# The first MLP product of a float32 encoder trunk: hi and lo activations as one 512-column moving operand, with one PSUM bank for each 128 features

## The chip, the cores and the metric

The kernel runs on one core of one Trainium2 chip. The metric is the device time of one execution in microseconds (us); smaller is better. TensorE is called PE in the rows below (PEld is its weight loading), VectorE is DVE, ScalarE is ACT, GpSimd is POOL and SyncE is SP.

## The reference

Two layers run on 256 tokens of 2048 features, all in float32. The attention part is cut here to its frame; what the change is about is the first product of the MLP, `h @ w_up`, and the square that follows it.

```python
for l in range(DEPTH):                                  # DEPTH = 2
    h = rmsnorm(x, norm_mix[l])
    proj = jnp.einsum('bsd,de->bse', h, w_in[l])
    ...                                                 # three attention groups A, B, C on parts of proj
    x = x + jnp.einsum('bse,ed->bsd', mix, w_o[l])
    h = rmsnorm(x, norm_mlp[l])
    u = jax.nn.relu(jnp.einsum('bsd,df->bsf', h, w_up[l]))      # 2048 -> 8192
    x = x + jnp.einsum('bsf,fd->bsd', u * u, w_down[l])         # 8192 -> 2048
return rmsnorm(x, norm_final)
```

## The kernel before

Every dense product is made exact enough by splitting both factors into two fp32r parts, hi and lo, and by summing three products: hi\*hi, hi\*lo and lo\*hi. Weights stream from memory in tiles of 512 KB (`wraw`, 6 buffers). ACT casts a tile to `whi` (L783), DVE subtracts to get `wlo` (L784); each of the two has four buffers. One such tile is one "step" of the program, and the steps form one long list that PE works through.

A step of the input projection, the output projection or the second MLP product (`mode_b`, L446 to L448) makes 12 matmuls of 512 columns: the activations stand in the array, and 512 columns of weights move. A step of the first MLP product (`up_steps`) is the other way round: 128x128 blocks of weights stand in the array, and the transposed activations of all 256 tokens move, so that the result comes out transposed, as the second product needs it. The activations of two blocks of 128 features lie in one tile `ht` of shape [128, 2 (hi, lo), 2 (block kk), 256 tokens]. For each block kk and each group `fs` of 128 output features there are three matmuls of 256 columns: hi weights by hi activations (L611), hi weights by lo activations (L612) and lo weights by hi activations (L613). That makes 24 matmuls in a step. Eight steps finish a chunk of 512 output features, which is held in two PSUM banks (two groups `fs` share a bank). At the end of a chunk each bank is emptied: ACT takes the relu (L617), POOL squares (L618), ACT casts the hi part (L621), and DVE subtracts to get the lo part (L622).

A layer has 16 chunks of the first product, hence 128 steps; the order is two chunks of the first product (16 steps), then 16 steps of the second product that use the results of the two chunks before, and so on. The two layers have 2 x 16 x 8 = 256 steps of the first product, with 256 x 8 = 2048 groups of three matmuls.

PSUM has eight banks. Six of them form one pool, `bank`, for matmul results and transposes; the two others hold the tile `S` of the attention scores (L318). What each engine does is in program order on that engine; the order is set when the program is built, by a scheduler that takes buffers from free pools. Attention pieces (scores, transposes of the weights L362, products with the values) are slipped in between dense steps by a planner with fixed costs and delays, which the change leaves as they are.

Of the kernel before, what the change touches and what calls it, by code (L numbers as in the profile page):

```python
"""Hybrid encoder trunk (three attention groups, squared-ReLU MLP) on one core.

Dense products run on the tensor engine as float32 split exactly into two fp32r
parts (hi + lo); hi*hi + hi*lo + lo*hi carries float32's accuracy in three passes.
The residual stream, attention and normalisations stay on chip; only weights stream.
"""
# [27 lines left out]
OUT_ORDER = "ACB"  # L34
# mixer feature blocks of 256 (two k-blocks each): A 0-1, B 2-3, C 4-7
GROUP_BLOCKS = {"A": (0, 1), "B": (2, 3), "C": (4, 5, 6, 7)}
# [7 lines left out]
def tile_trunk(ctx: ExitStack, tc: tile.TileContext, x_in, w_in, w_o, w_up, w_down,  # L44
# [28 lines left out]
    def mm_bank():  # L73
        return pp.tile([P, 512], F32, tag="bank", bufs=6, name=nm("mm"))

    def tr_bank():
        return pp.tile([P, 512], F32, tag="bank", bufs=6, name=nm("tr"))

# [1 line left out]
    ident = cp.tile([P, P], F32, name="ident")  # L80
# [25 lines left out]
    def setup_tables():  # L106
        """Rope tables with the gains folded in: out = x * ctab + swap16(x) * stab."""
        nc.vector.tensor_scalar(negsink, rp[:, :, 0:8], -1.0, None, op0=ALU.mult)
        for l in range(L):
            nc.vector.tensor_scalar(rp[:, l, 8:72], rp[:, l, 8:72], 0.125, None, op0=ALU.mult)  # L110
            for which, off in (("q", 8), ("k", 72)):
                g = rp[:, l:l + 1, off:off + 64]
                c = cp.tile([P, NT, 64], F32, name=f"ctab_{which}{l}")
                s = cp.tile([P, NT, 64], F32, name=f"stab_{which}{l}")
                nc.vector.tensor_mul(c, cos_t, g.to_broadcast([P, NT, 64]))
                for a in range(4):
                    b = a ^ 1
                    nc.vector.tensor_mul(s[:, :, 16 * a:16 * a + 16], sin_t[:, :, 16 * a:16 * a + 16],
                                         g[:, :, 16 * b:16 * b + 16].to_broadcast([P, NT, 16]))
                ctab[which, l], stab[which, l] = c, s  # L120

    def setup_avec():
        """Relative-position vector of group A, reversed: avec[h, i] = bias(h, rel = 255 - i)."""
        t5x = cp.tile([33, 8], F32, name="t5x")
# [12 lines left out]

# [1 line left out]
    bgq = []  # L139
# [7 lines left out]
    def add(fn, cost, after=(), delay=0):  # L147
        """Queue fn, `cost` us of PE time; it may start `delay` us from now or after the pieces in `after`."""
        p = Piece()
        p.fn, p.cost, p.after, p.delay, p.at, p.done = fn, cost, after, delay, cur[0], None  # L150
        bgq.append(p)
        return p
# [23 lines left out]

# [1 line left out]
    def hprep(key, gcol, j, hT, ss, done, fin_rs, late=0):  # L178
        """Column chunk j of x: partial sums of squares; k-blocks 4j..4j+3 of the operand."""
        def sq():  # L180
# [56 lines left out]

# [1 line left out]
    def q_transposes(src, pr0, qT):  # L239
        """src [P, t, heads*64]; 4 heads from pair pr0 -> qT [hi;lo, 4, 256]."""  # L240
        ps = tr_bank()
# [12 lines left out]
    def k_transposes(src, pr0, npr, kh, kl):  # L254
        """src [P, t, heads*64]; head pairs pr0.. -> hi/lo [every head in both halves, heads, 256]."""
        ps = tr_bank()
# [12 lines left out]
    def v_split(ps, parts, t, r):  # L269
        """Value columns of one bank, scaled, as hi/lo; parts: (first column, heads, tile)."""  # L270
        src = [ps[:, c0:c0 + nh * 64].rearrange("p (h d) -> p h d", h=nh) for c0, nh, _ in parts]
# [6 lines left out]
    def rope(raw, H, which, l, outs):  # L278
        """raw [P, t, H, 64]: per-head RMS norm, gain and axial rotary, in place of outs(t)."""
        n = NT * H  # L280
# [21 lines left out]

# [1 line left out]
    class Unit:  # L304
# [4 lines left out]
    def queue_unit(u, *preps):  # L309
        """Scores, transposes of the weights, product with the values; spaced for the softmax between."""  # L310
        after = list(preps) + last_s[-1:]
        sc = add(lambda: unit_scores(u), 0.87, after=after, delay=[D_S] * len(preps) + [D_SS])
        tr = add(lambda: unit_transp(u), 0.87, after=(sc,), delay=(D_T,))
        add(lambda: unit_pv(u), 0.87, after=(tr,), delay=(D_PV,))
        last_s.append(sc)

    def unit_scores(u):
        S = pp.tile([P, 4, 256], F32, tag="S", bufs=1, name=nm("S"))  # L318
        for s in range(4):
            qh, kh, qb = u.slot(s)  # L320
            st = u.qT[:, qh, qb * P:(qb + 1) * P]
            nc.tensor.matmul(S[:, s, :], st, u.kh[:, kh, :], start=True, stop=False)  # L322
            nc.tensor.matmul(S[:, s, :], st, u.kl[:, kh, :], start=False, stop=True)  # L323
        p = big(F32, 4, 256)
# [3 lines left out]
        if u.kind == "C":  # L328
            nc.vector.tensor_reduce(negm, S, axis=AX.X, op=ALU.max, negate=True)
            src = S  # L330
        else:
            for b in range(2):
                nc.vector.scalar_tensor_tensor(p[:, 2 * b:2 * b + 2, :], S[:, 2 * b:2 * b + 2, :], 0.125,
                                               u.bias(b), op0=ALU.mult, op1=ALU.add)
# [4 lines left out]
            else:  # L339
                nc.vector.tensor_reduce(negm, p, axis=AX.X, op=ALU.max, negate=True)  # L340
            src = p
        for s in range(4):
            nc.scalar.activation(p[:, s, :], src[:, s, :], AF.Exp, bias=negm[:, s:s + 1],
                                 accum_out=sums[:, s:s + 1])
# [53 lines left out]
    def mix_prep(l, grp, blk, raw, mixT, sqacc, done):  # L398
        """A finished block of 256 features: gained hi/lo operand and sum of squares."""
        m = big(F32R, 2, 2, 256)  # L400
# [30 lines left out]

# [1 line left out]
    steps = []  # L433
# [5 lines left out]
    def mode_b(banks, h_tile, wh, wl, sub, first, last, n=512, blocks=(0, 1)):  # L439
        """out[tok, n] += operand^T W over the tile's k-blocks."""  # L440
        for t in blocks:
# [10 lines left out]
    def layer_steps(l):  # L452
# [10 lines left out]

        # -- input projection --
        def proj_evac(name, banks):
# [93 lines left out]

        # -- output projection --  # L560
        st["hT2"], st["ss2"] = [None] * 8, small(8)
# [26 lines left out]

        # -- MLP --
        uT = {}  # L590

        def up_steps(g):
            for c in range(2):
                fc = 2 * g + c
                box = {}
                for k in range(8):
# [3 lines left out]
                    def mm(wh, wl, k=k, fc=fc, box=box):  # L600
                        if k == 0:
                            box["b"] = [mm_bank(), mm_bank()]
                        ht = st["hT2"][k]
                        for kk in range(2):
                            for fs in range(4):
                                o = box["b"][fs // 2][:, (fs % 2) * 256:(fs % 2) * 256 + 256]
                                s0 = k == 0 and kk == 0 and fs % 2 == 0
                                s1 = k == 7 and kk == 1
                                sh = wh[:, kk, fs * P:(fs + 1) * P]
                                sl = wl[:, kk, fs * P:(fs + 1) * P]  # L610
                                nc.tensor.matmul(o, sh, ht[:, 0, kk, :], start=s0, stop=False, skip_group_check=True)  # L611
                                nc.tensor.matmul(o, sh, ht[:, 1, kk, :], start=False, stop=False, skip_group_check=True)  # L612
                                nc.tensor.matmul(o, sl, ht[:, 0, kk, :], start=False, stop=s1, skip_group_check=True)  # L613
                        if k == 7:
                            for b in range(2):
                                a = mid(F32, 512)
                                nc.scalar.activation(a, box["b"][b], AF.Relu, bias=zero1[:, 0:1])  # L617
                                nc.gpsimd.tensor_mul(a, a, a)  # L618
                                u = big(F32R, 2, 2, 256)
# [54 lines left out]
    def final_chunk(j):  # L674
        """Squares of a finished column chunk; the final gain goes in ahead of the scale."""
        if not fin:
# [14 lines left out]
    def final_block(t):  # L691
        """Last chunk of token block t: norm over the whole row, scale, store."""
        square(3, t)
# [12 lines left out]

# [1 line left out]
    def bias_a(kv):  # L708
# [57 lines left out]

# [1 line left out]
    raw_t, hi_t, lo_t = {}, {}, {}  # L768
# [110 lines left out]
def _pack(w, nk):  # L879
    """[K, n] -> tiles [K/(128 nk), 128, nk*n]."""  # L880
    K, n = w.shape
# [61 lines left out]
```

## Time and profile before

| | |
|---|---|
| median of 3 runs | 2088.51 us (2088.35 to 2090.66) |
| span of the profiled execution | 2088.3 us |
| PE busy | 2066.0 us, 99% of the span |
| DVE busy | 1273.8 us, 61% |
| ACT busy | 1041.4 us, 50% |
| POOL busy | 340.1 us, 16% |
| mean granted TensorE clock | 0.997 of full speed |

The profiled execution's span lies 0.2 us below the median of the timed runs, so a time worked out from the span can be read as a time of a run. Matmuls are pipelined and overlap in the profile: a row says 0.28 us or 0.39 us for one, and the next starts much earlier. What a matmul costs is read from the starts of neighbouring rows, not from its length.

### The profile page before, as it was taken

What the parts mean: (1) busy time and instruction counts of PE and PEld (TensorE: products, weight loads), DVE (VectorE), ACT (ScalarE), POOL (GpSimd) and SP (SyncE); (2) the same over time, 40 slices, a digit from 0 to 9 for tenths busy, and PEclk for the clock granted to TensorE, in tenths of its full rate; (3) what the DMA queues carried; (4) which work ended last, traced back from release to release, by engine and by line L of the source; (5) the groups of instructions that cost most, each with busy time, mean ns of one, the idle gap of its engine ahead of it and who ended that gap; (6) DMA issues with size and microseconds to landing.
All of it is one profiled execution on the core that took longest, in us unless ns stands there. A gap on an engine that the chain in (4) does not pass through costs nothing.

```text
span 2088.3 us, 31322 instructions
## 1 busy us (share of the span) xinstructions
PE 2066.0 (99%) x12444; PEld 1847.9 (88%) x12444; DVE 1273.8 (61%) x1426; ACT 1041.4 (50%) x1472; POOL 340.1 (16%) x362
## 2 busy tenths in 40 slices
PE   9999999999999999999999999999999999999998
PEld 7878889989899898998888788899899898999986
DVE  6777976454555545555668789754555545555555
ACT  6657755444344444434556566554344444434444
POOL 0484420000000000000005844101000000000001
PEclk9999999999999999999999999999999999999999
DMA  8545455565655656556556453555655656565563
GB/s 289 179 160 157 155 185 176 183 192 180 194 186 187 192 183 192 187 188 189 188 177 188 141 170 130 180 174 181 194 188 183 192 189 191 184 192 185 190 212 121
DMA packets 107550, 381.49 MB, mean 183 GB/s; under 512 B 11875, under 2 KB 14691, under 8 KB 107404
## 3 DMA queue, kind: packets, MB, share of 16 engines
q1 hardware_dynamic: 107116, 378.45, 56.6%
q8 instruction: 97, 1.59, 0.3%
q10 hardware_dynamic: 288, 1.05, 0.1%
q14 instruction: 49, 0.40, 0.1%
HBM read 377.34 MB, written 2.11 MB: 182 GB/s over the span
## 4 chain that ended last, share of the span: by engine, by line
PE 94%; POOL 2%; DVE 1%; ACT 1%; issue 1%; DMA 0%; SPq 0%; POOLq 0%; DVEq 0%
PE mm L446 18%; PE mm L447 18%; PE mm L448 18%; PE mm L612 12%; PE mm L613 12%; PE mm L611 12%; PE tr L362 1%; PE tr L192 1%; PE tr L381 1%; PE S L323 1%; PE S L322 1%; POOL big L300 1%; POOL big L506 0%; PE tr L245 0%; POOL sm L235 0%
## 5 line engine op out<-in xcount | busy, mean ns | idle before, releaser
L784 DVE TENSOR_TENSOR wlo<-wraw,whi 128x1024 fp32r<-128x1024 f32 (+1 forms) x697 | 863.4, 1241 | 697.4 <-ACT whi L783 695.0
L783 ACT CAST whi<-wraw 128x1024 fp32r<-128x1024 f32 (+1 forms) x697 | 729.9, 1048 | 884.6 <-PE mm L448 473.0
L446 PE MATMUL mm<-whi,big 128*128 128x512 f32 (+1 forms) x1792 | 695.7, 389 | 3.1 <-DVE big L252 3.1
L447 PE MATMUL mm<-wlo,big 128*128 128x512 f32 (+1 forms) x1792 | 693.0, 387 | 0.0
L448 PE MATMUL mm<-whi,big 128*128 128x512 f32 (+1 forms) x1792 | 692.4, 386 | 0.0
L611 PE MATMUL mm<-big,whi 128*128 128x256 f32 x2048 | 579.8, 283 | 0.0
L613 PE MATMUL mm<-big,wlo 128*128 128x256 f32 x2048 | 579.6, 283 | 0.0
L612 PE MATMUL mm<-big,whi 128*128 128x256 f32 x2048 | 579.6, 283 | 0.0
L446 PEld LDWEIGHTS mm<-whi,big 128*128 128x128 f32 x1792 | 337.8, 189 | 68.1 <-issue 3.4
L448 PEld LDWEIGHTS mm<-whi,big 128*128 128x128 f32 x1792 | 337.4, 188 | 68.0
L447 PEld LDWEIGHTS mm<-wlo,big 128*128 128x128 f32 x1792 | 337.9, 189 | 64.8 <-DVE wlo L784 0.2
L612 PEld LDWEIGHTS mm<-big,whi 128*128 128x128 f32 x2048 | 393.2, 192 | 0.5
L611 PEld LDWEIGHTS mm<-big,whi 128*128 128x128 f32 x2048 | 393.1, 192 | 0.5
L613 PEld LDWEIGHTS mm<-big,wlo 128*128 128x128 f32 x2048 | 393.1, 192 | 0.0
L618 POOL TENSOR_TENSOR mid<-mid 128x512 f32<-128x512 f32 x64 | 74.2, 1159 | 1247.3 <-ACT mid L617 1247.3
L353 POOL TENSOR_SCALAR big<-big,sm 128x256 f32<-128x256 f32 x128 | 87.5, 701 | 230.3 <-DVE sm L351 164.3
L643 DVE SCALAR_TENSOR_TENSOR x<-mm,sm,x 128x512 f32<-128x512 f32 x128 | 89.9, 744 | 4.5 <-PE mm L448 4.5
L622 DVE TENSOR_TENSOR big<-mid,big 128x512 fp32r<-128x512 f32 x64 | 44.1, 689 | 50.7 <-ACT big L621 50.7
L621 ACT CAST big<-mid 128x512 fp32r<-128x512 f32 x64 | 39.8, 621 | 50.7 <-POOL mid L618 50.7
L617 ACT ACTIVATE mid<-mm,zero 128x512 f32<-128x512 f32 x64 | 43.8, 684 | 39.5 <-PE mm L613 39.5
L235 POOL TENSOR_TENSOR sm<-sm,mhalf 128x2 f32<-128x2 f32 (+3 forms) x16 | 24.7, 1547 | 131.0 <-DVE sm L230 117.0
L364 DVE TENSOR_TENSOR big<-tr,big 128x512 fp32r<-128x512 f32 x64 | 41.1, 680 | 0.3
(117 smaller groups left out, 1013.2 us busy)
## 6 DMA issues: line engine op xcount, KB each, us to landing
wraw<-in_w_up_dram SPq DMA_DIRECT2D x256, 512.0 KB, 4.3
wraw<-in_w_down_dram SPq DMA_DIRECT2D x256, 512.0 KB, 4.1
wraw<-in_w_in_dram SPq DMA_DIRECT2D x120, 512.0 KB, 3.3
wraw<-in_w_o_dram SPq DMA_DIRECT2D x64, 512.0 KB, 3.6
biasB<-in_rpb_dram SPq DMA_DIRECT2D x16, 349.5 KB, 6.2
biasA<-avec SPq DMA_DIRECT2D x4, 768.0 KB, 4.9
x<-in_x_dram SPq DMA_DIRECT2D x3, 512.0 KB, 9.1
big<-in_gfin_dram SPq DMA_DIRECT2D x2, 512.0 KB, 4.3
```

What stands on the lines that cost most here:

```text
L353: nc.gpsimd.tensor_scalar(p[:, s, :], p[:, s, :], rs[:, s:s + 1], 1.0, op0=ALU.mult, op1=ALU.mult)
L446: nc.tensor.matmul(o, a_h, wh[:, i, :], start=first and i == 0, stop=False)
L447: nc.tensor.matmul(o, a_h, wl[:, i, :], start=False, stop=False)
L448: nc.tensor.matmul(o, a_l, wh[:, i, :], start=False, stop=last and i == len(sub) - 1)
L611: nc.tensor.matmul(o, sh, ht[:, 0, kk, :], start=s0, stop=False, skip_group_check=True)
L612: nc.tensor.matmul(o, sh, ht[:, 1, kk, :], start=False, stop=False, skip_group_check=True)
L613: nc.tensor.matmul(o, sl, ht[:, 0, kk, :], start=False, stop=s1, skip_group_check=True)
L618: nc.gpsimd.tensor_mul(a, a, a)
L622: nc.vector.tensor_sub(uf[:, 1, :], a, f(uf[:, 0, :]))
L643: nc.vector.scalar_tensor_tensor(xs, box["b"][t], st["r2"][:, t:t + 1], xs, op0=ALU.mult, op1=ALU.add)
L783: last_hi[0] = nc.scalar.copy(h[:, part], w[:, part]).ins
L784: nc.vector.tensor_sub(lo[:, part], w[:, part], f(h[:, part]))
```

## The change

The two matmuls with the same hi weights (L611 and L612) become one: the hi and lo activations move as one operand of 2 x 256 columns, out of `ht[:, :, kk, :]`, whose two runs of 256 columns lie 512 elements apart. The result is 512 columns wide and fills a bank: columns 0 to 255 collect hi\*hi, columns 256 to 511 collect hi\*lo. The third matmul (lo weights by hi activations) is as before and adds to columns 0 to 255. So each `fs` has a bank of its own, a chunk has four banks, and the two halves of a bank are added at the end. ACT copies one half out, DVE adds the other, and DVE takes over relu and square in one instruction; POOL has no part in it any more. Each step has 16 matmuls in place of 24.

For the additional banks the tile `S` goes: the pool `bank` has all eight, and the scores take two banks of it. The operations on the scores are otherwise the same, but for the reduction of group C, which is made of two halves. All other lines of the difference are comments or follow from these (the exponentials read the halves where they lie).

```diff
     def mm_bank():
-        return pp.tile([P, 512], F32, tag="bank", bufs=6, name=nm("mm"))
+        return pp.tile([P, 512], F32, tag="bank", bufs=8, name=nm("mm"))
...
     def unit_scores(u):
-        S = pp.tile([P, 4, 256], F32, tag="S", bufs=1, name=nm("S"))
+        S = [mm_bank().rearrange("p (h c) -> p h c", h=2) for _ in range(2)]
...
         if u.kind == "C":
-            nc.vector.tensor_reduce(negm, S, axis=AX.X, op=ALU.max, negate=True)
+            for b in range(2):
+                nc.vector.tensor_reduce(negm[:, 2 * b:2 * b + 2], S[b], axis=AX.X, op=ALU.max, negate=True)
...
                         if k == 0:
-                            box["b"] = [mm_bank(), mm_bank()]
+                            box["b"] = [mm_bank() for _ in range(4)]
                         ht = st["hT2"][k]
                         for kk in range(2):
                             for fs in range(4):
-                                o = box["b"][fs // 2][:, (fs % 2) * 256:(fs % 2) * 256 + 256]
-                                s0 = k == 0 and kk == 0 and fs % 2 == 0
+                                o = box["b"][fs]
+                                s0 = k == 0 and kk == 0
...
-                                nc.tensor.matmul(o, sh, ht[:, 0, kk, :], start=s0, stop=False, skip_group_check=True)
-                                nc.tensor.matmul(o, sh, ht[:, 1, kk, :], start=False, stop=False, skip_group_check=True)
-                                nc.tensor.matmul(o, sl, ht[:, 0, kk, :], start=False, stop=s1, skip_group_check=True)
+                                nc.tensor.matmul(o.rearrange("p (s c) -> p s c", s=2), sh, ht[:, :, kk, :],
+                                                 start=s0, stop=False, skip_group_check=True)
+                                nc.tensor.matmul(o[:, 0:256], sl, ht[:, 0, kk, :],
+                                                 start=False, stop=s1, skip_group_check=True)
                         if k == 7:
                             for b in range(2):
+
                                 a = mid(F32, 512)
-                                nc.scalar.activation(a, box["b"][b], AF.Relu, bias=zero1[:, 0:1])
-                                nc.gpsimd.tensor_mul(a, a, a)
+                                for i in range(2):
+                                    o, ai = box["b"][2 * b + i], a[:, i * 256:(i + 1) * 256]
+                                    nc.scalar.copy(ai, o[:, 256:512])
+                                    nc.vector.tensor_add(ai, ai, o[:, 0:256])
+                                nc.vector.scalar_tensor_tensor(a, a, 0.0, a, op0=ALU.max, op1=ALU.mult)
```

On PE the first step of the second chunk (layer 0) stood like this before: three rows of 256 columns for each `fs`, `big` is the activations' tile, `mm` the bank.

```order
L611 MATMUL mm_705_3602<-big_630_3165,whi_696_3556 128x256
L612 MATMUL mm_705_3602<-big_630_3165,whi_696_3556 128x256
L613 MATMUL mm_705_3602<-big_630_3165,wlo_697_3557 128x256
L611 MATMUL mm_705_3602<-big_630_3165,whi_696_3556 128x256
L612 MATMUL mm_705_3602<-big_630_3165,whi_696_3556 128x256
L613 MATMUL mm_705_3602<-big_630_3165,wlo_697_3557 128x256
```

The same place in the changed program:

```order
L613 MATMUL mm_723_3570<-big_646_3189,whi_714_3526 128x512
L615 MATMUL mm_723_3570<-big_646_3189,wlo_715_3527 128x256
L613 MATMUL mm_724_3571<-big_646_3189,whi_714_3526 128x512
L615 MATMUL mm_724_3571<-big_646_3189,wlo_715_3527 128x256
L613 MATMUL mm_725_3572<-big_646_3189,whi_714_3526 128x512
```

Rows of 512 and of 256 columns now alternate, and the bank changes after every pair.

On DVE the end of the first chunk looked like this before. Call the chunk's last step s: `wlo_709` is the lo weights of step s+3, `wlo_712` those of s+4, and so on; the rows of L622 are the chunk's own.

```order
L784 TENSOR_TENSOR wlo_709_3631<-wraw_686_3464,whi_708_3630 128x1024
L784 TENSOR_TENSOR wlo_712_3661<-wraw_689_3494,whi_711_3660 128x1024
L622 TENSOR_TENSOR big_699_3587<-mid_698_3584,big_699_3587 128x512
L622 TENSOR_TENSOR big_701_3593<-mid_700_3590,big_701_3593 128x512
L784 TENSOR_TENSOR wlo_715_3691<-wraw_692_3524,whi_714_3690 128x1024
```

In the changed program `wlo_729` is that of step s+3, `wlo_732` of s+4, `wlo_735` of s+5:

```order
L791 TENSOR_TENSOR wlo_729_3593<-wraw_704_3458,whi_728_3592 128x1024
L624 TENSOR_TENSOR mid_716_3546<-mid_716_3546,mm_682_3342 128x256
L624 TENSOR_TENSOR mid_716_3546<-mid_716_3546,mm_683_3343 128x256
L624 TENSOR_TENSOR mid_718_3555<-mid_718_3555,mm_684_3344 128x256
L625 SCALAR_TENSOR_TENSOR mid_716_3546<-mid_716_3546 128x512
L791 TENSOR_TENSOR wlo_732_3615<-wraw_707_3480,whi_731_3614 128x1024
L629 TENSOR_TENSOR big_717_3552<-mid_716_3546,big_717_3552 128x512
L624 TENSOR_TENSOR mid_718_3555<-mid_718_3555,mm_685_3345 128x256
L625 SCALAR_TENSOR_TENSOR mid_718_3555<-mid_718_3555 128x512
L791 TENSOR_TENSOR wlo_735_3637<-wraw_710_3502,whi_734_3636 128x1024
```

Three additions and a relu-and-square stand in front of the lo weights of step s+4 now, and a subtraction, an addition and a second relu-and-square in front of those of step s+5.

On ACT, at the same place, the changed program has four short copies where two relus stood; the casts of the weights (L790, before L783) lie between them:

```order
L790 CAST whi_728_3592<-wraw_704_3458 128x1024
L623 COPY mid_716_3546<-mm_682_3342 128x256
L623 COPY mid_716_3546<-mm_683_3343 128x256
L623 COPY mid_718_3555<-mm_684_3344 128x256
L790 CAST whi_731_3614<-wraw_707_3480 128x1024
L623 COPY mid_718_3555<-mm_685_3345 128x256
L628 CAST big_717_3552<-mid_716_3546 128x512
```

The cast for step s+4 stands behind three of the copies, where before it stood behind one relu. In the attention stage PE's rows are the same as before, but for some transposes and single matmuls that moved by up to two dozen rows; POOL's rows there are the same.

## Rows read from the trace of the kernel before

**Rows 1.** The page: span, and each engine's busy us, share, instructions.

```profile
span 2088.3 us, 31322 instructions
...
PE 2066.0 (99%) x12444; PEld 1847.9 (88%) x12444; DVE 1273.8 (61%) x1426; ACT 1041.4 (50%) x1472; POOL 340.1 (16%) x362
...
PE   9999999999999999999999999999999999999998
...
PEclk9999999999999999999999999999999999999999
```

**Rows 2.** The page: chain that ended last, shares of the span.

```profile
PE 94%; POOL 2%; DVE 1%; ACT 1%; issue 1%; DMA 0%; SPq 0%; POOLq 0%; DVEq 0%
PE mm L446 18%; PE mm L447 18%; PE mm L448 18%; PE mm L612 12%; PE mm L613 12%; PE mm L611 12%; PE tr L362 1%; PE tr L192 1%; PE tr L381 1%; PE S L323 1%; PE S L322 1%; POOL big L300 1%; POOL big L506 0%; PE tr L245 0%; POOL sm L235 0%
```

**Rows 3.** Waits of PE and of its weight loading: us in total, times, longest.

```profile
PE tr L245 <- POOL big L506: 5.6, 2, 2.8
PE mm L446 <- DVE big L252: 3.1, 2, 1.5
...
PEld mm L447 <- DVE wlo L784: 0.2, 1, 0.2
```

**Rows 4.** The page: costliest groups, one line of the first product.

```profile
L611 PE MATMUL mm<-big,whi 128*128 128x256 f32 x2048 | 579.8, 283 | 0.0
```

**Rows 5.** Timeline of PE, borders of 16 first-product and 16 second-product steps: start, length.

```profile
553.93 0.39 PE L448 MATMUL mm<-whi,big 128*128 128x512 f32 x1
554.16 0.28 PE L611 MATMUL mm<-big,whi 128*128 128x256 f32 x1
...
600.11 0.28 PE L613 MATMUL mm<-big,wlo 128*128 128x256 f32 x1
600.23 0.40 PE L446 MATMUL mm<-whi,big 128*128 128x512 f32 x1
...
643.78 0.28 PE L611 MATMUL mm<-big,whi 128*128 128x256 f32 x1
```

**Rows 6.** Timeline of PE, attention scores between 512-column matmuls (layer 0).

```profile
92.24 0.39 PE L448 MATMUL mm<-whi,big 128*128 128x512 f32 x1
92.47 0.28 PE L322 MATMUL S<-mid,big 128*128 128x256 f32 x1
...
93.30 0.28 PE L323 MATMUL S<-mid,big 128*128 128x256 f32 x1
93.42 0.40 PE L446 MATMUL mm<-whi,big 128*128 128x512 f32 x1
```

**Rows 7.** Timeline of PE, transposes before a 512-column matmul (layer 0).

```profile
97.08 1.03 PE L362 MATMUL tr<-ident,big 128*128 128x128 f32 x8
...
97.87 0.48 PE L446 MATMUL mm<-whi,big 128*128 128x512 f32 x1
```

**Rows 8.** Groups by line and shape: busy us, mean ns, then idle before.

```profile
L618 POOL TENSOR_TENSOR mid<-mid 128x512 f32<-128x512 f32 x64 | 74.2, 1159 | 1247.3 <-ACT mid L617 1247.3
...
L622 DVE TENSOR_TENSOR big<-mid,big 128x512 fp32r<-128x512 f32 x64 | 44.1, 689 | 50.7 <-ACT big L621 50.7
L617 ACT ACTIVATE mid<-mm,zero 128x512 f32<-128x512 f32 x64 | 43.8, 684 | 39.5 <-PE mm L613 39.5
...
L201 DVE SCALAR_TENSOR_TENSOR big<-tr,gn,big 128x256 fp32r<-128x256 f32 x64 | 26.6, 477 | 7.7 <-ACT big L199 7.3 <-PE tr L192 0.4
L199 ACT ACTIVATE big<-tr,gn 128x256 fp32r<-128x256 f32 x64 | 25.3, 477 | 1.5 <-PE tr L192 1.5
...
L704 DVE SCALAR_TENSOR_TENSOR x<-x,sm,big 128x512 f32<-128x512 f32 x2 | 1.5, 746 | 0.0
```

**Rows 9.** Timeline of ACT and DVE behind a chunk's last step, which ends at 600.23.

```profile
600.31 1.05 ACT L783 CAST whi<-wraw 128x1024 fp32r<-128x1024 f32 x1
601.39 1.23 DVE L784 TENSOR_TENSOR wlo<-wraw,whi 128x1024 fp32r<-128x1024 f32 x1 [1.66 <-ACT whi L783]
```

More of the change, by code (lines that the diff above doesn't have):

```diff
@@ L73, in mm_bank @@
     def mm_bank():
-        return pp.tile([P, 512], F32, tag="bank", bufs=6, name=nm("mm"))
+        return pp.tile([P, 512], F32, tag="bank", bufs=8, name=nm("mm"))
     def tr_bank():
-        return pp.tile([P, 512], F32, tag="bank", bufs=6, name=nm("tr"))
+        return pp.tile([P, 512], F32, tag="bank", bufs=8, name=nm("tr"))
     ident = cp.tile([P, P], F32, name="ident")
@@ L321, in unit_scores @@
             st = u.qT[:, qh, qb * P:(qb + 1) * P]
-            nc.tensor.matmul(S[:, s, :], st, u.kh[:, kh, :], start=True, stop=False)
-            nc.tensor.matmul(S[:, s, :], st, u.kl[:, kh, :], start=False, stop=True)
+            o = S[s // 2][:, s % 2, :]
+            nc.tensor.matmul(o, st, u.kh[:, kh, :], start=True, stop=False)
+            nc.tensor.matmul(o, st, u.kl[:, kh, :], start=False, stop=True)
         p = big(F32, 4, 256)
@@ L328, in unit_scores @@
         if u.kind == "C":
-            nc.vector.tensor_reduce(negm, S, axis=AX.X, op=ALU.max, negate=True)
-            src = S
+            for b in range(2):
+                nc.vector.tensor_reduce(negm[:, 2 * b:2 * b + 2], S[b], axis=AX.X, op=ALU.max, negate=True)
+            src = [S[s // 2][:, s % 2, :] for s in range(4)]
         else:
             for b in range(2):
-                nc.vector.scalar_tensor_tensor(p[:, 2 * b:2 * b + 2, :], S[:, 2 * b:2 * b + 2, :], 0.125,
+                nc.vector.scalar_tensor_tensor(p[:, 2 * b:2 * b + 2, :], S[b], 0.125,
                                                u.bias(b), op0=ALU.mult, op1=ALU.add)
@@ L340, in unit_scores @@
                 nc.vector.tensor_reduce(negm, p, axis=AX.X, op=ALU.max, negate=True)
-            src = p
+            src = [p[:, s, :] for s in range(4)]
         for s in range(4):
-            nc.scalar.activation(p[:, s, :], src[:, s, :], AF.Exp, bias=negm[:, s:s + 1],
+            nc.scalar.activation(p[:, s, :], src[s], AF.Exp, bias=negm[:, s:s + 1],
                                  accum_out=sums[:, s:s + 1])
```

## The prediction

> **What bounds the kernel now.** I read the page's totals first: PE is busy for 2066.0 us of a span of 2088.3 us, its strip of forty slices is full but for the last, and the granted clock's strip is full throughout [rows 1]. A full busy strip alone doesn't prove that PE is the bound, since pipelined matmuls overlap in the profile. So the chain comes next: PE holds 94% of it, and the three lines of the first MLP product hold 12% each [rows 2]. Then PE's waits: the two largest belong to attention (5.6 us behind the rotary products on POOL, 3.1 us behind DVE), and in the whole execution the weight loading waits for the lo weights once, 0.2 us [rows 3]. In the MLP nothing but PE's own rate sets the time. What a change is worth there is therefore what it does to the distance between the starts of neighbouring matmuls; work that it adds on ACT and DVE costs only if it makes PE wait.
>
> **The rate of the two shapes.** The timeline of PE gives it over long stretches. Sixteen steps of the first product go from 554.16 to 600.23 [rows 5]: 46.07 us for 16 x 24 = 384 matmuls of 256 columns, 120.0 ns each. The sixteen steps of the second product that follow go to 643.78: 43.55 us for 16 x 12 = 192 matmuls of 512 columns, 226.8 ns each. Two matmuls of 256 columns take 240.0 ns, and one of 512 columns takes 226.8: the merge saves 13.2 ns, a cost that each matmul has whatever its width. The row of line L611 says that there are 2048 such matmuls [rows 4]; its mean of 283 ns is a length with overlap and isn't used.
>
> Does the distance depend on the neighbour, since the change makes the two shapes alternate? The borders say no, to the 10 ns that the rows resolve: a 512-column matmul followed by a 256-column one took 0.23 us (553.93 to 554.16, and 92.24 to 92.47), a 256-column one followed by a 512-column one took 0.12 us (600.11 to 600.23, and 93.30 to 93.42) [rows 5, 6]. Each matmul takes what its own width takes.
>
> **The change part by part.**
>
> *PE, first product.* For each weight block three matmuls at 120.0 ns (360.0) become one at 226.8 and one at 120.0 (346.8): 13.2 ns less. With 2048 of them: 27.0 us. The columns moved are the same 768, and the weight load that falls away lay beside the matmuls. The bounds: no group can fall under its columns' time, and the fixed cost that goes is one of three, so the saving isn't above 27 us by more than the reading error (0.01 us at both ends of each stretch, nothing). Downward the one new thing is the moving operand in two runs of 256 columns, 512 elements apart; no row of before has one. Its cost lies between zero and what the slowest row gives: eight transposes of 128 columns took from 97.08 to 97.87 [rows 7], 99 ns each, 0.77 ns for a column against 0.44 here. At that rate 512 columns take 395 ns, 168 more than reckoned. I take zero: within each run the columns lie as in the rows of 512, and the change of run comes once.
>
> The Trainium skill (TensorE: Matmul & The Clock Gate, Back-to-back issue gap) gives another size for the merge: a gap of columns/2.4 plus about 2.5 ns, by which two matmuls of 256 columns lose only 2.5 ns when they become one. By that figure 2048 merges would save 5.1 us and the time would be an estimated 2083 us. This case's rows show 13.2 ns [rows 5], and they are for this kernel's own operands and weight loads, so the measured number stands in the sum.
>
> *Emptying the banks, on ACT and DVE.* A chunk has two relus of 512 columns (684 ns each), two squares on POOL (1159) [rows 8]; it gets four ACT copies and four DVE additions of 256 columns, for which the nearest rows are the scalings of 256 columns out of PSUM (477 ns on either engine), and two relu-and-squares of 512 columns in DVE, nearest L704 with 746 ns [rows 8]. Over 32 chunks: ACT 128 x 0.477 - 43.8 = +17 us; DVE 128 x 0.477 + 64 x 0.746 = +109 us; POOL -74.2 us. DVE goes from 61% to some 67% of the span, ACT to 51%. The cast and the subtraction (L621, L622) stay. None of it is on the path if the lo weights still come in time, and that is the cover to check. At the chunk end of 600.23 the cast for step s+4 began at 600.31, and the subtraction ran from 601.39 to 602.62 [rows 9]; four buffers for `whi` and `wlo` are why it can't begin before step s is done. PE needs it with the second matmul of step s+4, three steps of 2.72 us and 0.23 us later, at 608.6: 6.0 us to spare. After the change three additions and one relu-and-square stand ahead of it on DVE, three copies ahead of the cast on ACT. The four banks are complete at 5/8, 6/8, 7/8 and 8/8 of the last step (2.77 us then), that is 1.04, 0.69, 0.35 and 0 us before its end. Taken from the end, with 0.16 us for the matmul to finish: copies end at -0.41, 0.07 and 0.54, the cast at 1.6; the additions end at 0.07, 0.55 and 1.0, the relu-and-square at 1.8, and the lo weights of s+4 at 3.0 in place of 2.4. So 0.6 of 6.0 us are used. Those of s+5 come behind one more subtraction, addition and relu-and-square at about 6.2, needed at 11.1. Then the queue is level again, since a step of 2.77 us has only 1.23 us of weights on DVE. Cost on the path: zero. Without the cover each us by which the queue is later than that margin costs 32 us.
>
> *Other things behind the same steps.* Results of a chunk are first needed by the second product, at least eight steps later, so a slower emptying reaches nobody. Four banks of eight are filled while the four others empty for a whole chunk (8 x 2.77 = 22 us against some 5 us). The weight loads keep their number, and a step of 2.77 us asks less of them than the 2.72 us that the second product's steps have now [rows 5].
>
> *Attention.* The scores leave their own two banks for the common pool, group C's reduction becomes two (at most 1.2 us more of DVE for each of 16 units), and a few transposes move by up to two dozen rows on PE. PE's waits there are 5.6 and 3.1 us in total for both layers [rows 3], two waits of each kind. A moved row can take away one of those or add another of that size, so plus or minus 5 us; I take zero.
>
> *Sum.* 2088.3 - 27.0 = 2061.3 us of span; the median of the runs lies 0.2 us above the profiled span, so 2061.5 us.
>
> **The rivals.**
>
> *The second run has a start of its own.* If the array begins the second run of the operand as it begins a matmul, each merged matmul takes 2 x 120 = 240 ns and the change does nothing: 2088.5 us. A start that costs only part of it gives 2061.5 + 2.05 us for each ns. For it: no row shows such an operand. Against it: the 13.2 ns go with a matmul and its weight load, and the second run has neither. The skill's 2.5 ns would be a case of small saving like this one. Chance 0.06.
>
> *The second run is read slowly.* Above 13.2 ns for a merged matmul the change loses; at the transposes' rate it is 168 ns and 2048 x 0.168 = 344 us, some 2405 us. The Trainium skill (Advanced Engine Details and Errata, Memory Cachelines) has a penalty for accesses that change the 16-byte line each time; runs of 256 float32 lie in whole lines, so by that rule nothing is lost here, and no row of before tests it. Chance 0.03.
>
> *DVE becomes late.* If the emptying holds the queue for four times what I reckon, the lo weights of s+4 arrive after 608.6. From 0.84 us of stall in each of the 32 chunks on (27.0 / 32) the kernel is slower than before; with 1.5 us it is 2061.5 + 48 = 2109 us. For it: DVE's new work stands ahead of the weights in strict order. Against it: 6.0 us to spare. Chance 0.03.
>
> **How the numbers follow.** The forecast has 0.88, of which some 0.78 lies within 2055 to 2068: the attention's 5 us on either side, and half a ns for each pair of distances (1 us). To hold 8 in 10 the range goes a little into the partial start of the first rival, to 2071 (5 ns for a merged matmul). A measurement of this kernel tells about 0.2% (4 us) from no change. Faster: the forecast and the half of the first rival that keeps more than 2 ns, 0.91. Same: the rest of that rival and a small stall, 0.04. Slower: 0.05.
>
> **What would show it.** In the profile after, starts in the first product should lie 0.23 and 0.12 us apart in turn, and a pair of chunks (16 steps) should take 44.4 us in place of 46.07. The matmul count falls by 2048, POOL loses 74 us, DVE gains about 109. PE's waits should still not name the lo weights. I'd be wrong if the 512-column rows of the first product lie further apart than those of the second, or if PE shows waits behind DVE at chunk ends.

## The result and the profile after

The changed kernel takes 2077.26 us (median of 4 runs, 2077.01 to 2079.79) against 2089.59 us for the kernel before (4 runs, 2088.35 to 2090.74): a ratio of 0.9944 (95% interval 0.9930 to 0.9959). It is faster by some 12 us (0.6%). The forecast was 27 us, to 2061.5 us, and the result lies outside the range that was given.

The page of the changed kernel, its totals, the strip of the granted clock and the chain of waits:

```profile
span 2078.0 us, 27361 instructions
...
PE 2054.5 (99%) x10396; PEld 1736.4 (84%) x10396; DVE 1359.5 (65%) x1634; ACT 1045.0 (50%) x1536; POOL 274.6 (13%) x298
...
PEclk9999999999999999999999999999999999999999
...
PE 93%; DVE 3%; POOL 2%; issue 1%; ACT 0%; DMA 0%; SPq 0%; POOLq 0%; DVEq 0%
```

Beside [rows 1, 2] PE still holds the chain at an unchanged clock, with 2048 matmuls fewer (12444 to 10396). POOL lost 65.5 us, DVE gained 85.7, ACT 3.6. The profiled run is the longest of the four (2079.79 us, 1.8 us above its span); sums below are made from span to span, 2088.3 to 2078.0, a gain of 10.3 us.

The groups by line; the first two are the merged matmul and its narrow neighbour, then the copies, the additions and the relu-and-square of the emptying (busy us, mean ns, then idle before):

```profile
L613 PE MATMUL mm<-big,whi 128*128 128x512 f32 x2048 | 724.4, 399 | 0.0
...
L615 PE MATMUL mm<-big,wlo 128*128 128x256 f32 x2048 | 575.1, 281 | 0.0
...
L623 ACT COPY mid<-mm 128x256 f32<-128x256 f32 x128 | 46.6, 373 | 26.7 <-PE mm L615 26.7
L624 DVE TENSOR_TENSOR mid<-mid,mm 128x256 f32<-128x256 f32 x128 | 49.4, 419 | 0.0
L625 DVE SCALAR_TENSOR_TENSOR mid<-mid 128x512 f32<-128x512 f32 x64 | 44.0, 688 | 1.1
```

PE's waits:

```profile
PE tr L245 <- POOL big L508: 5.5, 2, 2.8
PE tr L192 <- DMA x<-in_x_dram: 3.9, 2, 3.3
PE tr L383 <- DVE big L366: 1.7, 4, 0.6
...
PE mm L448 <- DVE x L585: 1.0, 2, 0.5
PE mm L323 <- DVE mid L396: 1.0, 2, 0.5
PE mm L449 <- DVE wlo L791: 0.4, 2, 0.2
```

No line of the first product (L613, L615) waits, and the lo weights are late twice, by 0.2 us, both times outside it. So what is missing in the first product is no wait for another engine. It has to lie in the distances between matmuls, and the timeline of PE shows it there, in the same stretch as [rows 5] (16 steps of the first product, then the second product's first row):

```profile
553.20 0.39 PE L613 MATMUL mm<-big,whi 128*128 128x512 f32 x1
553.43 0.28 PE L615 MATMUL mm<-big,wlo 128*128 128x256 f32 x1
...
554.25 0.40 PE L613 MATMUL mm<-big,whi 128*128 128x512 f32 x1
554.49 0.28 PE L615 MATMUL mm<-big,wlo 128*128 128x256 f32 x1
554.60 0.40 PE L613 MATMUL mm<-big,whi 128*128 128x512 f32 x1
...
598.29 0.28 PE L615 MATMUL mm<-big,wlo 128*128 128x256 f32 x1
598.41 0.40 PE L448 MATMUL mm<-whi,big 128*128 128x512 f32 x1
```

From 553.20 to 598.41 are 45.21 us for 128 pairs, 353.2 ns a pair. Before, three matmuls took 359.9 ns; the forecast was 346.8 (44.4 us). The first pair of the stretch, right behind 512-column matmuls, still starts 0.23 us apart; from a few pairs on it is mostly 0.24 (554.25 to 554.49). A merge saves 6.7 ns, not 13.2.

### The profile page after: what moved, and what is told of

The parts are those of the page before. It is cut to its first block, busy times and chain, and to the rows that moved or that the text cites. A ratio compares the mean times of both kernels' runs of the same rounds, so it can differ in the third digit from the quotient of the medians.

```text
span 2078.0 us, 27361 instructions
## 1 busy us (share of the span) xinstructions
PE 2054.5 (99%) x10396; PEld 1736.4 (84%) x10396; DVE 1359.5 (65%) x1634; ACT 1045.0 (50%) x1536; POOL 274.6 (13%) x298
## 4 chain that ended last, share of the span: by engine, by line
PE 93%; DVE 3%; POOL 2%; issue 1%; ACT 0%; DMA 0%; SPq 0%; POOLq 0%; DVEq 0%
PE mm L613 23%; PE mm L449 18%; PE mm L448 18%; PE mm L450 18%; PE mm L615 12%; PE tr L364 1%; PE tr L192 1%; DVE wlo L791 1%; PE mm L323 1%; PE mm L324 1%; DVE big L267 1%; POOL big L300 1%; PE tr L383 0%; POOL big L508 0%; POOL sm L235 0%
## 5 line engine op out<-in xcount | busy, mean ns | idle before, releaser
L790 ACT CAST whi<-wraw 128x1024 fp32r<-128x1024 f32 (+1 forms) x697 | 731.3, 1051 | 914.4 <-PE mm L450 477.3
L613 PE MATMUL mm<-big,whi 128*128 128x512 f32 x2048 | 724.4, 399 | 0.0
L615 PE MATMUL mm<-big,wlo 128*128 128x256 f32 x2048 | 575.1, 281 | 0.0
L613 PEld LDWEIGHTS mm<-big,whi 128*128 128x128 f32 x2048 | 384.8, 188 | 95.8
L615 PEld LDWEIGHTS mm<-big,wlo 128*128 128x128 f32 x2048 | 386.8, 189 | 0.5
L355 POOL TENSOR_SCALAR big<-big,sm 128x256 f32<-128x256 f32 x128 | 96.0, 767 | 224.7 <-DVE sm L353 200.0
L691 POOL TENSOR_TENSOR x<-x,big 128x512 f32<-128x512 f32 x6 | 8.6, 1456 | 722.6 <-ACT mid L695 722.6
L623 ACT COPY mid<-mm 128x256 f32<-128x256 f32 x128 | 46.6, 373 | 26.7 <-PE mm L615 26.7
L624 DVE TENSOR_TENSOR mid<-mid,mm 128x256 f32<-128x256 f32 x128 | 49.4, 419 | 0.0
L625 DVE SCALAR_TENSOR_TENSOR mid<-mid 128x512 f32<-128x512 f32 x64 | 44.0, 688 | 1.1
L366 DVE TENSOR_TENSOR big<-tr,big 128x512 fp32r<-128x512 f32 x64 | 41.1, 680 | 0.8 <-ACT big L365 0.5
```

The costliest lines, as they stand in the source:

```text
L355: nc.gpsimd.tensor_scalar(p[:, s, :], p[:, s, :], rs[:, s:s + 1], 1.0, op0=ALU.mult, op1=ALU.mult)
L613: nc.tensor.matmul(o.rearrange("p (s c) -> p s c", s=2), sh, ht[:, :, kk, :], start=s0, stop=False, skip_group_check=True)
L615: nc.tensor.matmul(o[:, 0:256], sl, ht[:, 0, kk, :], start=False, stop=s1, skip_group_check=True)
L623: nc.scalar.copy(ai, o[:, 256:512])
L624: nc.vector.tensor_add(ai, ai, o[:, 0:256])
L625: nc.vector.scalar_tensor_tensor(a, a, 0.0, a, op0=ALU.max, op1=ALU.mult)
```

## Experiments

The measure in all of them is the distance of starts in one stretch of 16 steps with nothing else in it, because a pair's few ns add up 128 times there. Of kernels that change the first product (before and after beside them):

| order in the first product (columns) | 16 steps, us | ns for each weight block |
|---|---|---|
| before: 256, 256, 256 | 46.07 | 359.9 |
| after: 512, 256 in turn | 45.21 | 353.2 |
| e1: as after, operand in one run | 45.21 | 353.2 |
| e2: four of 512, four of 256 | 44.88 | 350.6 |
| e3: 256, 256, 256, rest as after | 46.08 | 360.0 |
| e5: all 512 | 58.03 | 453.4 (226.7 each) |
| e6, e12: two of 512, two of 256 | 44.58 | 348.3 |
| e9: eight of 512, eight of 256 | 44.66 | 348.9 |
| e10: four and four, banks in pairs | 44.88 | 350.6 |
| e11: fours across the steps | 44.90 | 350.8 |
| sum of the uniform rates, 226.7 + 120.0 | 44.4 | 346.7 |

The letters in the quoted expectations name theories, among them A, that each of the two runs of the operand costs; B, that each change of width costs; C and D, that a change of the bank costs; F, that a wide matmul costs more when weights stand and activations move; B', that the excess goes with the changes of width, but not in proportion; R, that neighbours with the same bank or moving operand matter. The runs are told in the order in which they were made.

**e1: the operand in one run.** `ht` is laid out as [P, kk, (hi, lo), 256], so that hi and lo of a block lie side by side.

```diff
...
-nc.tensor.matmul(o.rearrange("p (s c) -> p s c", s=2), sh, ht[:, :, kk, :],
+nc.tensor.matmul(o, sh, ht[:, kk, :, :].rearrange("p s c -> p (s c)"),
...
```

> The changed kernel, with only the layout of the activations' tile altered, so that hi and lo of one block lie next to each other and the 512 columns are one run. In the changed kernel a pair (512 and 256 columns) takes 353.3 ns from start to start of the next pair, where the rows of before give 346.7. Theory A (the second run of the operand costs some 6.6 ns in each merged matmul): the pair falls to 346.7 ns, 16 steps of the first product take 44.4 us, and the time falls by 2048 x 6.6 ns = 13.5 us, to about 2063 us. Theory B (alternating widths cost it) and theory C (a change of bank after each pair costs it): the pair stays at 353.3 ns and the time at about 2077 us.

Measured: 2076.89 us (5 runs, 2076.40 to 2078.98), ratio 0.9935 (0.9921 to 0.9948), the same as with two runs. The stretch on the timeline of PE:

```profile
553.98 0.39 PE L616 MATMUL mm<-big,whi 128*128 128x512 f32 x1
...
599.19 0.40 PE L451 MATMUL mm<-whi,big 128*128 128x512 f32 x1
```

45.21 us, to the hundredth that of after. The two runs cost nothing; the first rival, which would have given a time of this size, is not the cause.

**e2: widths grouped.** For each kk four 512-column matmuls, then the four of 256.

```diff
+for part in range(2):
     for fs in range(4):
...
+        if part == 0:
             nc.tensor.matmul(o.rearrange("p (s c) -> p s c", s=2), sh, ht[:, :, kk, :], ...)
+        else:
             nc.tensor.matmul(o[:, 0:256], sl, ht[:, 0, kk, :], ...)
```

> The changed kernel, with the four 512-column matmuls of a block first and the four 256-column ones behind them; operands, layout and banks as in the changed kernel. Theory A (second run): a step stays at 8 x 353.3 = 2.83 us and the 512-column rows lie some 233 ns apart. Theory B (alternating widths): three of four 512-column rows lie 226.7 ns apart, three of four 256-column rows 120 ns, and a step falls to about 2.79 us. Theory C (change of bank): the bank now changes after every matmul, so the pair rises to about 360 ns and a step to 2.88 us.

Measured: 2072.67 us, span 2070.9; 44.88 us for the 16 steps. Changing the order alone gains. The timeline of PE (four rows of a kind in one line):

```profile
551.85 1.09 PE L615 MATMUL mm<-big,whi 128*128 128x512 f32 x4
552.78 0.63 PE L618 MATMUL mm<-big,wlo 128*128 128x256 f32 x4
553.25 1.09 PE L615 MATMUL mm<-big,whi 128*128 128x512 f32 x4
```

Four wide ones take 0.93 us (232 ns each, 6 above their uniform rate), four narrow ones 0.47 (118, 2 below theirs). The wide ones are the slow ones, and no longer only at a border. It gained less than a cost for each change of width would have given back.

**e3: everything but the merge.** Four banks, the new emptying and the pool of eight stay; the merged matmul becomes two of 256 columns into the halves of its bank.

```diff
-nc.tensor.matmul(o.rearrange("p (s c) -> p s c", s=2), sh, ht[:, :, kk, :], ...)
+nc.tensor.matmul(o[:, 0:256], sh, ht[:, 0, kk, :], ...)
+nc.tensor.matmul(o[:, 256:512], sh, ht[:, 1, kk, :], ...)
```

> The changed kernel, with the merged matmul made as two matmuls of 256 columns again, into the two halves of the same bank; four banks, the new emptying and the scores' banks stay. Theories A and B: each matmul takes 120.0 ns, a step 2.88 us, and the span is that of before within 3 us (2088 us), which also prices the rest of the change. Theory C (change of bank after each group costs 6.6 ns): a group of three takes 366.6 ns and the span is some 2102 us.

Measured: 2092.02 us, span 2090.2, beside 2090.9 (2088.36 to 2091.48) for the kernel before; 120.0 ns for each matmul, though the bank changes as in after. So the change of banks costs nothing with equal widths. The rest of the change adds 1.9 us from span to span, no more than the spread of the runs of before; the part of it that is a cost is worked out behind the experiments, under attention.

**e4: two runs in the second product.** Kernel before, with each 512-column operand of the second product taken as two runs of 256.

```diff
+def mv(w, i=i):
+    return w.rearrange("p k (h c) -> p k h c", h=2)[:, :, i, :] if runs else w[:, i, :]
...
-nc.tensor.matmul(o, a_h, wh[:, i, :], ...)
+nc.tensor.matmul(ov, a_h, mv(wh), ...)
```

> The kernel before, with only the moving operand of the second MLP product altered: its 512 columns of weights are taken as two runs of 256, 512 elements apart (first halves of both blocks, then second halves; so it multiplies other pairs than the reference, with the same number of instructions, columns and banks). Theory A: the 3072 matmuls of that product go from 226.7 ns to some 233 ns apart, and the span rises by 3072 x 6.6 ns = 20 us to about 2108 us. Theories B and C: 226.7 ns as before and a span of 2088 us.

Measured: 2091.67 us, span 2089.9. The 16 steps of the second product go from 512.06 to 555.61, 43.55 us, as in [rows 5]. With e1 this settles that the two runs are free, in either product.

**e5: one width only.** After, with the third matmul made 512 columns wide too.

```diff
-nc.tensor.matmul(o[:, 0:256], sl, ht[:, 0, kk, :],
+nc.tensor.matmul(o.rearrange("p (s c) -> p s c", s=2), sl, ht[:, :, kk, :],
```

> The changed kernel, with the third matmul also 512 columns wide (lo weights by hi and lo activations, so lo*lo is added): in the first product every matmul is 512 wide, two in a row go to one bank. Theory B (a change of width costs some 3.3 ns, two of them in each pair): no widths change, so 226.7 ns for each, a pair 453.4 ns. Theory D (a 512-column matmul costs more when the bank changes behind it): 453.4 + 6.6 = 460 ns. Theory F (a 512-column matmul with weights standing and activations moving takes 233 ns or more): a pair 466 ns or more. The span rises by some 2048 x 100 to 113 ns, 205 to 231 us above that of the changed kernel (2078 us).

Measured: 2281.42 us, span 2279.6. Its timeline of PE:

```profile
488.95 0.39 PE L613 MATMUL mm<-big,whi 128*128 128x512 f32 x1
...
546.98 0.39 PE L448 MATMUL mm<-whi,big 128*128 128x512 f32 x1
```

58.03 us for 256 matmuls, 226.7 ns each. The operand with two runs, the banks and the turns of hi and lo weights are those of after, and the excess is gone: it needs two widths.

**e6: two and two.** For each bank the two 512-column matmuls (kk = 0, 1), then its two of 256.

```diff
-for kk in range(2):
-    for fs in range(4):
+for fs in range(4):
+    for kk in range(2):
...
         nc.tensor.matmul(o.rearrange("p (s c) -> p s c", s=2), sh, ht[:, :, kk, :], ...)
+    for kk in range(2):
...
         nc.tensor.matmul(o[:, 0:256], sl, ht[:, 0, kk, :], ...)
```

> The changed kernel, with the matmuls of a step ordered by bank: for each of the four banks two of 512 columns (both blocks), then two of 256. Widths change twice in two pairs, the bank once in two pairs. Theory B: 346.7 + 3.3 = 350.0 ns for a pair, a step 2.80 us. Theory D: 512 followed by 256 in the same bank, so the excess halves or goes, 346.7 to 350 ns. Theory F: 353.3 ns as in the changed kernel.

Measured: 2067.9 us, span 2066.1; 348.3 ns for a pair. That is less than with four and four, although the width changes twice as often: a fixed cost for each change of width doesn't hold.

**e7: mixed widths in the second product.** Kernel before, the third of each three matmuls cut to 256 columns (`n3=256`).

```diff
-nc.tensor.matmul(o, a_l, wh[:, i, :], ...)
+nc.tensor.matmul(o[:, 0:n3 or n], a_l, wh[:, i, 0:n3 or n], ...)
```

> The kernel before, with only the third matmul of the second MLP product cut to 256 columns (it leaves out half of the lo*hi product): there widths run 512, 512, 256 in one bank, with weights moving. By the rows of before three take 226.7 + 226.7 + 120.0 = 573.4 ns. Theory B: two changes of width add 6.6 ns, 580 ns. Theories D and F: 573.4 ns. The span falls by 1024 x 106.7 = 109 us, or by 102 us under theory B (to 1979 or 1986 us).

Measured: 1992.54 us, span 1990.8, slower than either figure expected. The second product's 16 steps go from 503.10 to 540.64, 37.54 us for 64 groups of three: 586.6 ns, where the uniform rates give 2 x 226.7 + 120.0 = 573.4. The excess is 13.2 ns a group, twice that of after, with other weights, another operand and one bank for a whole group. It isn't peculiar to the first product.

**e8: banks in turn, one width.** Kernel before, the second product changes bank after every matmul.

```diff
+for i, kk in enumerate(sub):
+    for q in range(3):
+        for t in blocks:
+            a = h_tile[i][:, int(q == 2), kk, t * P:(t + 1) * P]
+            nc.tensor.matmul(banks[t][:, 0:n], a, (wh, wl, wh)[q][:, i, :], ...)
```

> The kernel before, with only the order of the second MLP product altered: its two banks take turns after every matmul of 512 columns. Theories B and F: 226.7 ns each, span 2088 us. Theory D: 233 ns each, 3072 x 6.6 = 20 us more, span 2108 us.

Measured: 2090.44 us, span 2088.7; its 16 steps go from 510.89 to 554.44, 43.55 us. Nothing lost: alternating banks are free here too.

**e9: eight and eight.** All wide matmuls of a step, then all narrow ones.

```diff
+order = [(w, fs, kk) for w in (1, 0) for kk in range(2) for fs in range(4)]
```

> The changed kernel, with the eight 512-column matmuls of a step first and its eight 256-column ones behind them, bank by bank in turn: two changes of width in a step. Uniform rates would make the step 8 x 346.7 = 2.773 us; so far a step takes 2.826 (pairs), 2.805 (four and four, a new bank after each matmul) and 2.786 us (two and two in one bank). Theory B' (the excess belongs to the changes of width, whatever their number costs): two changes leave at most a quarter of the excess of the pairs, 2.78 to 2.79 us. Theory R (in a mixed stretch it is a new bank, or the shared moving operand, that costs): as many new banks as in the four-and-four order, so 2.80 us or more.

Measured: 2069.16 us, span 2067.4; 348.9 ns. The timeline of PE:

```profile
552.73 2.00 PE L614 MATMUL mm<-big,whi 128*128 128x512 f32 x8
554.57 1.12 PE L617 MATMUL mm<-big,wlo 128*128 128x256 f32 x8
555.53 2.00 PE L614 MATMUL mm<-big,whi 128*128 128x512 f32 x8
```

The eight wide ones take 1.84 us (230 ns each, 26 ns more in all than 8 x 226.7), the eight narrow ones 0.96 (120). So the cost stands behind a change from narrow to wide, and it is spread over several wide matmuls. Eight and eight have one such change in a step, turns have eight.

**e10: four and four with the banks in pairs.** Four wide matmuls into two banks, then their four narrow ones.

```diff
+order = [(w, fs, kk) for h in (0, 2) for w in (1, 0) for fs in (h, h + 1) for kk in range(2)]
```

> The changed kernel, in the order four of 512, four of 256, with each bank visited twice in a row (two blocks): as many changes of width as the four-and-four order with 2.805 us a step, half as many new banks, and the moving operand alternates. Theory B': the same changes of width, 2.80 us. Theory R: 2.786 us or less, since the bank stays for two matmuls.

Measured: 2072.38 us, span 2070.6; 44.88 us for 16 steps, that of e2. So half as many new banks, and a moving operand that alternates, gain nothing. From e6 it still differs in two things: the order of the widths, and that in e6 a bank stays for four matmuls.

**e11: the order turned round for every second bank.** Wide, narrow, narrow, wide.

```diff
+order = [(w, fs, kk) for fs in range(4) for w in ((1, 0), (0, 1))[fs % 2] for kk in range(2)]
```

> The changed kernel, ordered by bank as the two-and-two kernel, with every second bank taking its 256-column matmuls first, so that widths run 2, 4, 4, 4, 2: four changes of width in a step in place of eight. Theory B': less than the two-and-two order, some 2.78 us a step and a time of about 2066 us. Theory R: the bank changes as in the two-and-two order, 2.786 us and about 2068 us.

Measured: 2071.58 us (4 runs, 2071.03 to 2072.82), ratio 0.9912 (0.9897 to 0.9927). A miss: it is no better than four and four. Read as a sequence, narrow and wide ones now follow one another in fours, and the rate is that of fours (350.8 ns beside 350.6), although a bank stays for four matmuls as in e6. So of all that differs between e2 and e6 only the order of the widths is left.

**e12: two and two, timed.** The kernel of e6 again, with more runs.

> The two-and-two kernel again (for each bank two matmuls of 512 columns, then two of 256), timed. Its single execution took 2067.9 us, which the 5 ns that its pair is shorter (2048 x 5 = 10 us) explain beside the changed kernel's 2077 us. Expected 2067 us, ratio to before 0.989; if the single look was luck, 2077 us.

Measured: 2068.69 us (4 runs, 2067.95 to 2070.05), ratio 0.9900 (0.9883 to 0.9916): the best version that was timed in several runs, some 9 us below the change as it was made (ratio 0.9944). Its stretch on the timeline of PE:

```profile
550.16 0.61 PE L610 MATMUL mm<-big,whi 128*128 128x512 f32 x2
...
551.54 0.63 PE L610 MATMUL mm<-big,whi 128*128 128x512 f32 x2
552.00 0.40 PE L614 MATMUL mm<-big,wlo 128*128 128x256 f32 x2
552.24 0.63 PE L610 MATMUL mm<-big,whi 128*128 128x512 f32 x2
...
594.74 0.40 PE L448 MATMUL mm<-whi,big 128*128 128x512 f32 x1
```

44.58 us: the two wide ones take 0.46, the two narrow ones 0.24, 1.6 ns a pair more than the uniform rates.

## Why the prediction was wrong, and where it was right

**The step that failed** is "Each matmul takes what its own width takes", and with it the term 13.2 ns x 2048 = 27.0 us. The two rates are right where a width stands alone: e5 gives 226.7 ns, e3 120.0, so merging with nothing else beside it would be worth 13.3 ns. In turn with a narrow matmul a merge is worth 6.7. One sign of being wrong that the prediction named came true: the first product's 512-column rows lie further apart than the second's, mostly 0.24 us.

The trace of before already held the warning. At each border I had read the last matmul ahead of it, to 10 ns, and 0.23 and 0.12 us looked like each width's own; no wide matmul that stands behind a narrow one was among them. The timeline of the kernel before, right behind the border at 600.23 [rows 5], shows more:

```profile
600.47 0.40 PE L447 MATMUL mm<-wlo,big 128*128 128x512 f32 x1
600.70 0.39 PE L448 MATMUL mm<-whi,big 128*128 128x512 f32 x1
...
601.39 0.39 PE L448 MATMUL mm<-whi,big 128*128 128x512 f32 x1
...
602.30 0.39 PE L446 MATMUL mm<-whi,big 128*128 128x512 f32 x1
```

From 600.23 to 602.30 are nine wide matmuls in 2.07 us, 230 ns each, like the eight of e9: the first five take 1.16 us (232 each), the next four 0.91 (228). In before that happens once in 16 steps and drowns in the mean of 226.8; in after it is the whole product.

**The sum, mended.** In the profile after, twelve stretches of 16 steps fell from 46.07 to 45.21 us, and two of 31 steps (at the head of each layer's MLP, behind its first step) from 89.35 to 87.70: 12 x 0.86 + 2 x 1.65 = 13.6 us in place of 27.0. What is left to explain of the 10.3 us of span is a loss of 3.3. The last step of the sum, 0.2 us from span to run, is off as well, but small: each run lies 1.8 us above its own span (2079.79 and 2078.0), and the 0.2 came of setting one execution's span beside the median of three runs.

**Attention, taken as 0 with 5 either way**, is most of it. The rows with which the 31-step stretches of the two layers start, and between them the last border of layer 0, before:

```profile
331.64 0.36 PE L611 MATMUL mm<-big,whi 128*128 128x256 f32 x1
...
958.71 0.40 PE L446 MATMUL mm<-whi,big 128*128 128x512 f32 x1
...
1365.68 0.36 PE L611 MATMUL mm<-big,whi 128*128 128x256 f32 x1
```

and after:

```profile
333.13 0.47 PE L613 MATMUL mm<-big,whi 128*128 128x512 f32 x1
...
953.58 0.40 PE L448 MATMUL mm<-whi,big 128*128 128x512 f32 x1
...
1361.93 0.47 PE L613 MATMUL mm<-big,whi 128*128 128x512 f32 x1
```

Layer 0 reaches this stretch 1.5 us later; from 958.71 and 953.58 layer 1 takes 406.97 and 408.35 us, 1.4 more. The remaining 0.4 is in the second product (43.58 us for 16 steps, before 43.55), whose wide matmuls now follow another neighbour. The bound of 5 us held.

The other traces bear out the 1.4 us, if runs with the same granted clock are compared. In layer 1's attention PE waits 2.7 us behind POOL (L245); behind that wait the granted clock fell from 2.4 to 1.2 GHz for a short while in most traces (in after, 512-column matmuls start 0.43 us apart there, at 1158.79 and 1159.22), but not in e1, e3, e5 and e11 (e1 has the same wait, 2.8 us). The stretch from 1145 to 1170 us in before, after and e1: busy us of PE, PEld, DVE, ACT and POOL, then the mean granted clock, 0.93, 0.93 and 1.00, and the DMA.

```profile
1145.00:1170.00 25.00, 22.22 (x100) 18.27 (x101) 21.18 (x24) 14.10 (x21) 20.70 (x19) 0.93 0.40 134
1145.00:1170.00 25.00, 22.28 (x102) 18.52 (x101) 19.63 (x23) 12.62 (x18) 19.49 (x19) 0.93 0.39 121
1145.00:1170.00 25.00, 22.22 (x111) 18.53 (x110) 21.26 (x25) 13.36 (x18) 20.58 (x19) 1.00 0.43 138
```

With the fall, layer 1's distance is 406.97 to 407.10 us in the old attention (before, e4, e8) and 408.35 to 408.42 in the new (after, e2, e6, e9, e10, e12); without it the new one takes 406.78 to 406.86 (e1, e3, e11); e5 and e7 have other matmuls in this stretch. So at the same clock the new attention costs 1.4 us a layer, and the fall some 1.6, enough to hide it. Which of the moved pieces makes the 1.4 us no run parts. PE's own waits cancel: 3.1 us behind L252 [rows 3] and 0.9 behind L470 are gone, 1.7 behind L366, 1.0 each behind L585 and L396 and 0.4 behind the lo weights are new. Those of the weight loading grew, most of all before the transposes, here before and after:

```profile
PEld tr L381 <- DVE big L364: 1.4, 4, 0.4
...
PEld tr L383 <- DVE big L366: 4.6, 8, 1.0
```

**The emptying**, costed at nothing, is right: it makes no wait in the first product. The chunk whose last step ends at 598.41, on DVE:

```profile
597.96 1.13 DVE L624 TENSOR_TENSOR mid<-mid,mm 128x256 f32<-128x256 f32 x3
599.01 0.68 DVE L625 SCALAR_TENSOR_TENSOR mid<-mid 128x512 f32<-128x512 f32 x1
599.62 1.23 DVE L791 TENSOR_TENSOR wlo<-wraw,whi 128x1024 fp32r<-128x1024 f32 x1
```

The lo weights of step s+4 end 2.44 us behind the chunk (600.85), where I had put 3.0 and before had 2.39 (602.62 [rows 9]). The cover wasn't needed. The prices were too high: an addition takes 419 ns (I took 477), a relu-and-square 688 (746), a copy 373 (477), so ACT's 17 us became 4. For DVE they give 98 us where I took 109; its busy time, in which overlapping rows count once, rose by 86.

**The rivals.** The second run's own start would have given nearly the time measured, with 6.5 ns in each pair (2061.5 + 13.4 us), but e1 and e4 refute it: a right size from a cause that isn't there. A slow second run falls with it, and a late DVE is refuted by the waits. The case that came true, a cost between neighbours of different width, I had asked about and closed with four readings, all of the matmul ahead of a border, so it got no chance.

The Trainium skill (TensorE: Matmul & The Clock Gate, Back-to-back issue gap) puts some 2.5 ns on a matmul whatever its width, as the gap of an isolated one. The 2083 us worked out from it lay 6 us above the time measured, nearer than the forecast (16 below), but not for its reason: with equal widths the runs show 13.3 ns (e3, e5), and the rest is the mixing.

**Shown**: the excess needs both widths, it goes with their order, it falls on the wide matmuls behind a change from narrow to wide, and neither the operand's two runs, nor the banks, nor the product, nor which factor moves makes it. **Open**: what in TensorE makes it, and why runs of two (1.6 ns a pair) do better than turns (6.5), fours (3.9) and eights (2.3). No run here looked inside the engine. Each matmul also brings a weight load of its own, and no run parts the two, so whether the loads have a share in it isn't shown.

## What to carry to other kernels

A rate read from a uniform stretch holds for that stretch: before adding two of them up, read eight or ten instructions behind a border and divide, not the one interval at it. Where matmuls of two widths share a loop, their order is a free parameter worth trying; here two and two in place of turns gained some 9 us more beside the 12 of the change. When parts of a few us are compared between traces, the granted clock has to be compared stretch by stretch: the page's strip of forty slices was full in before and after, and the fall was in both. A time that fits one's rival is no proof of it: e1 and e4, a few lines each, took that story away.

## What the hardware showed that was not expected

- Matmuls of 512 and 256 columns in one stream cost more than the sum of their uniform rates: 6.5 ns a pair in turn, 13.2 ns for 512, 512, 256 in the second product.
- The dependence on the order isn't monotonic: per pair 353.2 (ones), 348.3 (twos), 350.6 (fours), 348.9 ns (eights).
- After a change to 512 columns eight matmuls took 230 ns each in place of 226.7 (e9); in before the first five of them took 232, the next four 228.
- A moving operand in two runs of 256 columns, 512 elements from start to start, cost nothing measurable (e1, e4), nor did a change of bank after every matmul (e8) or after every group of equal widths (e3, e5).
